# Six edits to the order of work around the FFNs, the first convolution steps on ScalarE, and the length of two down parts

## The chip, the cores and the metric

The kernel runs on one core of a Trainium2 chip. The metric is the device time of one execution in microseconds (us); lower is better. PE is TensorE, DVE VectorE, ACT ScalarE, POOL GpSimd, SP SyncE, which issues nearly all DMAs. A difference under 0.2% (6.8 us) can't be told from none here.

## The reference

Three parts, each over S = 1024 tokens of D = 1024 features in float32:

```python
for layer in range(2):                         # first block
    y = conv_lru_mixer(x) if layer == 0 else diff_attention_mixer(x)
    x = layer_norm(ALPHA * x + y)
    x = layer_norm(ALPHA * x + (silu(x @ w_gate) * (x @ w_up)) @ w_down)    # D_FF = 2816
mod = c_act @ w_ada + b_ada                    # second block: six rows of 1024
h = ln(x) * (1 + sc1) + sh1
x = ln_affine(ALPHA * x + (1 + g1) * (concat(mlstm(h), fourier(h)) @ w_out))
h2 = ln(x) * (1 + sc2) + sh2
out = ln_affine(ALPHA * x + (1 + g2) * (square(relu(h2 @ w_ff1 + b_ff1)) @ w_ff2 + b_ff2))  # 4096
```

The first mixer's A half is a causal depthwise convolution with 31 taps, over a gated projection, then a layer norm and silu; its B half a convolution with 4 taps before a gated linear recurrence.

## The kernel before

A class `Net` records all operations; a scheduler of the framework then sets each engine's order by its own costs, so the program's order is a wish and priority. Dependencies are kept by semaphores. Features lie on the 128 partitions; eight tiles of 128 tokens (`NTT = 8`).

**Matmuls.** Each float32 product is made of three matmuls. `split` (L213, L214) casts a tile to a rounded high part on ScalarE and subtracts it on VectorE for the low part; `mm3` (L235 to L237) multiplies high by high, low by high, high by low. A weight of 128x1024 is loaded to a `raw` buffer (a ring of three, `self.rp`), cast to `wh`, split to `wl`.

**The first mixer.** `conv` (L482 to L486) makes one half of a chunk: a first step `co = ga * w + b`, then 30 steps `co += shifted ga * w`, all on VectorE; 8 halves. `taps` (L503 to L506) does the same with 4 taps for 4 chunks `rc`. `prod_a` transposes `co` into `pt` (L576) and on.

**Gate and up.** They are made in pairs of features by seven products instead of eight, in `product` (L697 on). `prepare` makes from two weight tiles the combinations S1 to S4 (L674 to L677 on VectorE, then casts and splits); `xn.sums` (L150 to L153) makes from the tokens the combinations T1 to T4, where T1 to T4 of the second token half need the last tile. In `product`: `corner` A11B11 into `wx`, kept by a copy `keep`; S2T2 into `wy`, plus `keep`, copied to `u`; S1T1 into `wz`, copied to `p5`, plus `u`; S3T3 added into `wy`; `sum22` adds `wy` and `p5`; `corner2` A12B21 added into `wx`; S4B22 into `wz`; A22T4 into `wy`. Each of these terms is 12 matmuls. `start` begins the corner products of six pieces already while the mixer ends (`more` in the pipes of the three stages before; `EARLY` gives how many per call), since they need no sums.

**Down.** `run_ffn` makes the second product in parts of features: `PARTS1` for the first two FFNs, `PARTS2` for the third. For a part, `weights(j)` loads, casts and splits the weights of its features; kind "x" keeps them in tiles `wd` of the pool of 16 KB tiles, "u" in `wh`, `wl` of the large pool. Then for each token tile `tokens` loads the activations back from `hd` as `ht` (four features a load), `down_tile` multiplies into `dn`, and `add` adds that to `xr` (L898). The next part's weights come after the third tile (`WAHEAD`). In the last part, norm, transposes and the next stage's products follow in a pipe. In the second FFN, a side job runs along: `steps` issues w_ada loads of 512 KB, each followed by one reduction on VectorE (L1240), 48 in all, `SD` per product and `SDN` per down tile.

**Third FFN.** Its gate is `square(relu)`, L1821 on ScalarE and L1822 on VectorE. Its down weights are scaled by a row (L1828), and a bias row `b2` is scaled once (L1836) and added to each tile in its second part (L1844), both on GpSimd.

## Time and profile before

| | |
|---|---|
| median of 3 runs | 3423.69 us (3421.68 to 3425.16) |
| profiled execution | 3421.3 us, span 3419.5 us |
| mean granted clock of TensorE | 0.985 |
| PE busy | 3269.5 us, 96% |
| VectorE busy | 2185.5 us, 64% |
| ScalarE busy | 1412.9 us, 41% |
| GpSimd busy | 265.6 us, 8% |
| DMA share of 16 engines | 30.6%, 348.68 MB |

Times are us from the span's start. The first mixer lies at 0 to 370, the first FFN's gate and up to 758, its down to about 1040, attention to 1610, the second FFN's gate and up to 2055, its down with the second block's first norms to 2345, the second block's mixer to 2745, the third FFN's gate and up to 3054, its down to the end. PE is nearly full, so its gaps are what is read. A wait row names the waiting engine, tile and line, then the engine, tile and line that ended the wait. Where a wait is for several, it is put down to the one that came last.

### The profile page before, as it was taken

What the parts mean: (1) busy time and instruction counts of PE and PEld (TensorE: products, weight loads), DVE (VectorE), ACT (ScalarE), POOL (GpSimd) and SP (SyncE); (2) the same over time, 40 slices, a digit from 0 to 9 for tenths busy, and PEclk for the clock granted to TensorE, in tenths of its full rate; (3) what the DMA queues carried; (4) which work ended last, traced back from release to release, by engine and by line L of the source; (5) the groups of instructions that cost most, each with busy time, mean ns of one, the idle gap of its engine ahead of it and who ended that gap; (6) DMA issues with size and microseconds to landing.
All of it is one profiled execution on the core that took longest, in us unless ns stands there. A gap on an engine that the chain in (4) does not pass through costs nothing.

```text
span 3419.5 us, 40944 instructions
## 1 busy us (share of the span) xinstructions
PE 3269.5 (96%) x15588; PEld 2692.5 (79%) x15588; DVE 2185.5 (64%) x3445; ACT 1412.9 (41%) x2422; POOL 265.6 (8%) x458
## 2 busy tenths in 40 slices
PE   8998999999999999989999999999999989999998
PEld 7776788878877878877788878778777878878887
DVE  8997755555357677676765558654446876566635
ACT  4455433332237667655533332224334554432211
POOL 1011000000020111101000000013001300000201
PEclk9999999999999999999999999999999999999999
DMA  3131322235312111141332238721123333344312
GB/s 126 42 112 62 101 91 74 91 128 169 106 62 71 36 50 50 43 149 56 109 107 99 93 120 290 237 74 47 59 84 106 116 117 117 116 161 165 113 51 79
DMA packets 191764, 348.68 MB, mean 102 GB/s; under 512 B 14384, under 2 KB 105936, under 8 KB 191568
## 3 DMA queue, kind: packets, MB, share of 16 engines
q1 hardware_dynamic: 191568, 346.07, 30.6%
q8 instruction: 122, 2.00, 0.2%
q14 instruction: 74, 0.61, 0.1%
HBM read 268.41 MB, written 72.36 MB: 100 GB/s over the span
## 4 chain that ended last, share of the span: by engine, by line
PE 66%; DVE 13%; ACT 9%; DMA 5%; issue 4%; POOL 3%; SPq 0%; POOLq 0%; DVEq 0%; ACTq 0%
PE dn L236 6%; PE dn L235 6%; PE dn L237 6%; PE wy L235 4%; PE wy L236 4%; PE wy L237 4%; PE wx L235 3%; PE wx L237 3%; PE wx L236 3%; PE pi L235 3%; PE pi L236 3%; PE pi L237 2%; PE wz L235 2%; PE wz L237 2%; PE wz L236 2%
## 5 line engine op out<-in xcount | busy, mean ns | idle before, releaser
L213 ACT CAST wh<-raw 128x1024 fp32r<-128x1024 f32 (+1 forms) x275 | 282.7, 1048 | 405.1 <-DVE raw L677 138.1
L214 DVE TENSOR_TENSOR wl<-raw,wh 128x1024 fp32r<-128x1024 f32 (+1 forms) x275 | 334.3, 1233 | 132.1 <-ACT wh L213 128.1
L213 ACT CAST ht<-ht 128x512 fp32r<-128x512 f32 (+1 forms) x168 | 97.2, 580 | 448.0 <-DMA ht<-hd 438.7
L235 PE MATMUL dn<-wd,ht 128*128 128x512 f32 x704 | 274.4, 391 | 3.3 <-ACT wd L213 3.3
L236 PE MATMUL dn<-wd,ht 128*128 128x512 f32 x704 | 274.8, 390 | 1.3 <-DVE wd L214 1.2
L237 PE MATMUL dn<-wd,ht 128*128 128x512 f32 x704 | 274.4, 390 | 0.0
L235 PE MATMUL dn<-wh,ht 128*128 128x512 f32 x512 | 200.9, 392 | 10.8 <-DVE xr L898 6.7
L214 DVE TENSOR_TENSOR ht<-ht 128x512 fp32r<-128x512 f32 (+1 forms) x168 | 112.3, 673 | 153.2 <-ACT ht L213 152.4
L235 PE MATMUL wx<-bh,wh 128*128 128x512 f32 x480 | 192.2, 400 | 10.6 <-ACT keep L693 4.2
L237 PE MATMUL wx<-bh,wl 128*128 128x512 f32 x480 | 190.2, 397 | 11.2 <-DVE wl L214 11.2
L237 PE MATMUL dn<-wh,ht 128*128 128x512 f32 x512 | 200.3, 391 | 0.4 <-DVE ht L214 0.4
L236 PE MATMUL dn<-wl,ht 128*128 128x512 f32 x512 | 200.2, 391 | 0.0
L236 PE MATMUL wx<-bl,wh 128*128 128x512 f32 x480 | 190.3, 396 | 0.0
L235 PE MATMUL pi<-xh,wh 128*128 128x512 f32 x416 | 168.8, 406 | 7.8 <-DVE xl L214 7.8
L486 DVE SCALAR_TENSOR_TENSOR co<-ga,col,co 128x512 f32<-128x512 f32 (+18 forms) x240 | 165.4, 737 | 0.5
L237 PE MATMUL pi<-xh,wl 128*128 128x512 f32 x416 | 165.0, 397 | 0.0
L236 PE MATMUL pi<-xl,wh 128*128 128x512 f32 x416 | 164.9, 396 | 0.0
L235 PEld LDWEIGHTS dn<-wd,ht 128*128 128x128 f32 x704 | 132.3, 188 | 32.0 <-ACT wd L213 4.6
L236 PEld LDWEIGHTS dn<-wd,ht 128*128 128x128 f32 x704 | 132.4, 188 | 30.3 <-DVE wd L214 2.9
L237 PEld LDWEIGHTS dn<-wd,ht 128*128 128x128 f32 x704 | 132.4, 188 | 27.5
L287 POOL TENSOR_SCALAR nm<-sum 128x1 f32<-128x1 f32 x47 | 15.1, 322 | 1562.8 <-DVE xr L898 1323.1
L898 DVE SCALAR_TENSOR_TENSOR xr<-xr,dn 128x1024 f32<-128x1024 f32 x64 | 77.8, 1216 | 85.5 <-PE dn L237 81.3
(458 smaller groups left out, 8446.4 us busy)
## 6 DMA issues: line engine op xcount, KB each, us to landing
raw<-w_gu SPq DMA_DIRECT2D x100, 512.0 KB
hd<-g SPq DMA_DIRECT2D x152, 256.0 KB
raw<-w_f SPq DMA_DIRECT2D x70, 512.0 KB
ht<-hd SPq DMA_DIRECT2D x136, 256.0 KB
raw<-w_ada SPq DMA_DIRECT2D x48, 512.0 KB
raw<-w_dn SPq DMA_DIRECT2D x44, 512.0 KB
raw<-w_in SPq DMA_DIRECT2D x26, 512.0 KB
raw<-w_out SPq DMA_DIRECT2D x24, 512.0 KB
```

What stands on the lines that cost most here:

```text
L213: self.nc.scalar.copy(hi, src)
L214: (self.nc.gpsimd if pool else self.nc.vector).tensor_sub(lo, src, hi.bitcast(F32))
L235: mm(out, l[0], r[0], start=first, stop=False, **kw)
L236: mm(out, l[0], r[1], start=False, stop=False, **kw)
L237: mm(out, l[1], r[0], start=False, stop=last, **kw)
L287: (nc.vector if NMV else nc.gpsimd).tensor_scalar(nm, a, -1.0 / D, None, op0=ALU.mult)
L486: nc.vector.scalar_tensor_tensor(co[c][:, a:hi_], ga[c][:, a - s:hi_ - s], self.c("conv_w", 31 * c + 30 - s), co[c][:, a:hi_], op0=ALU.mul ...
L898: nc.vector.scalar_tensor_tensor(xr[i], xr[i], DN_ALPHA if first else 1.0, p, op0=ALU.mult, op1=ALU.add, accum_out=self.sum_of(xr[i]) if l ...
```

## The change

- A. The first step of `conv` and of `taps` is an activation (Identity with scale and bias) on ScalarE instead of a `tensor_scalar` on VectorE.
- B. In the pipes ahead of the three gate/up stages, `more` for the last tile stands ahead of `sums`.
- C. In `product`, `corner2` stands ahead of S3T3 instead of after `sum22`.
- D. `weights(0)`, the first down weights of each FFN, is called ahead of the last product instead of after it.
- E. `PARTS1` goes from 8x, 6u, 4x, 4u to 8x, 4u, 4x, 6u.
- F. The last part's `ht` in the first two FFNs comes from the `raw` ring of three instead of the large pool.
- G. `SDN`, w_ada steps per down tile, goes from 2 in all parts to 3, 1, 1, 0 by part.
- H. In the third FFN the scaling of `b2` and its eight additions go from GpSimd to VectorE.

```diff
@@ -28,7 +28,7 @@
 NF2 = 4096 // P
 NEG = -1.0e30
 EARLY, WAHEAD = (1, 1, 2, 2), 2
-PARTS1 = ((8, "x"), (6, "u"), (4, "x"), (4, "u"))
+PARTS1 = ((8, "x"), (4, "u"), (4, "x"), (6, "u"))
 PARTS2 = ((8, "x"), (6, "u"), (8, "x"), (6, "u"), (4, "x"))
 L2 = 2
 DV = 1
@@ -48,7 +48,7 @@
 WE, WP = 0, (0, 1)
 LM, MF, AF2, TF2 = 5, (3,4,5), (0,1,2), True
 NDB = (4, 4, 4, 4, 2, 2, 2, 2)
-SD, SDN, KA, KB = (0, 1), 2, 1, 3
+SD, SDN, KA, KB = (0, 1), (3, 1, 1, 0, 0), 1, 3
 FA, FB, FC = (3, 3, 3, 4, 4, 3, 2, 2), (4, 4, 4, 4, 1, 2, 2, 2), (2, 2, 2, 2, 1, 1, 1, 1)
 ND2 = (2,) * 8
 TS, TS0, TSM, T2 = True, False, True, 3
@@ -479,8 +479,8 @@
 
         def conv(c, h):
             lo_, hi_ = h * H512, (h + 1) * H512
-            nc.vector.tensor_scalar(co[c][:, lo_:hi_], ga[c][:, lo_:hi_], self.c("conv_w", 31 * c + 30),
-                                    self.c("conv_b", c), op0=ALU.mult, op1=ALU.add)
+            nc.scalar.activation(co[c][:, lo_:hi_], ga[c][:, lo_:hi_], AF.Identity, bias=self.c("conv_b", c),
+                                 scale=self.c("conv_w", 31 * c + 30))
             for s in range(1, 31):
                 a = max(lo_, s)
                 nc.vector.scalar_tensor_tensor(
@@ -500,8 +500,7 @@
         def taps(c):
             rec = recs[c]
             rc = rcs[c] = self.u("rc")
-            nc.vector.tensor_scalar(rc, rec, self.c("lconv_w", 4 * c + 3), self.c("lconv_b", c),
-                                    op0=ALU.mult, op1=ALU.add)
+            nc.scalar.activation(rc, rec, AF.Identity, bias=self.c("lconv_b", c), scale=self.c("lconv_w", 4 * c + 3))
             for s in range(1, 4):
                 nc.vector.scalar_tensor_tensor(rc[:, s:], rec[:, :S - s], self.c("lconv_w", 4 * c + 3 - s),
                                                rc[:, s:], op0=ALU.mult, op1=ALU.add)
@@ -632,7 +631,7 @@
             conv(c, 1)
         more = lambda i: start() if i == NTT - 1 else None
         self.pipe(pre + [(0, lambda i: feat(i - 4)), (LE, prod_a), (LE + ME[0], more), (LE + ME[1], more),
-                         (LE + ME[2], more), (LE + 1, norm), (LE + 2, feat), (LE + 3, xn.sums), (LE + 3, more)],
+                         (LE + ME[2], more), (LE + 1, norm), (LE + 2, feat), (LE + 3, more), (LE + 3, xn.sums)],
                   range(4, 8))
 
     def mixer_end(self, xr, xn, layer):
@@ -712,10 +711,10 @@
         p5 = self.tmp("p5")
         nc.scalar.copy(p5, pz)
         nc.vector.tensor_add(pz, pz, u2)
+        if not early:
+            self.corner2(o, x, px, finish)
         self.term(py, o["S3"], x, "T3", False, True)
         sum22(py, p5)
-        if not early:
-            self.corner2(o, x, px, finish)
         self.term(pz, o["S4"], x, "B22", False, True)
         finish(0, 1, pz)
         self.term(py, o["A22"], x, "T4", False, True)
@@ -788,20 +787,6 @@
         def prep(n):
             q, m = order[n]
             return self.prepare(src(2 * q, m), src(2 * q + 1, m), first=(q, m) not in started)
-
-        o = prep(0)
-        while begun:
-            finish_first()
-        for n, (q, m) in enumerate(order):
-            nxt = prep(n + 1) if n + 1 < len(order) else None
-            finish, sum22 = finisher(q, m)
-            self.product(o, x, keep(q, m), finish, sum22, (q, m) in started)
-            if m == nm - 1:
-                ctx.pop(q)
-            if n % 2:
-                kept.pop(n // 2)
-            o = nxt
-            steps(SD[n % 2])
 
         def weights(j):
             n, kind = parts[j]
@@ -818,13 +803,30 @@
                 ws.append((t[:, e, :], t[:, e + 1, :]))
             return ws
 
+        ws = {}
+        o = prep(0)
+        while begun:
+            finish_first()
+        for n, (q, m) in enumerate(order):
+            nxt = prep(n + 1) if n + 1 < len(order) else None
+            finish, sum22 = finisher(q, m)
+            if nxt is None:
+                ws[0] = weights(0)
+            self.product(o, x, keep(q, m), finish, sum22, (q, m) in started)
+            if m == nm - 1:
+                ctx.pop(q)
+            if n % 2:
+                kept.pop(n // 2)
+            o = nxt
+            steps(SD[n % 2])
+
         def tokens(j, i):
             n, hs = parts[j][0], []
             for a in range(0, n, 4):
                 e = min(n, a + 4)
                 shape = (P, 2, e - a, P)
                 if add_half is None and j == len(parts) - 1:
-                    t = self.u("ht", shape, F32R)
+                    t = self.rp.tile(list(shape), F32R, tag="raw", name=self.name("ht"))
                 else:
                     t = self.wp.tile(list(shape), F32R, tag="w", name=self.name("ht"))
                 raw = t[:, 1].bitcast(F32)
@@ -834,7 +836,7 @@
             return hs
 
         todo = [(j, i) for j in range(len(parts)) for i in range(NTT)]
-        ws, hs = {0: weights(0)}, {}
+        hs = {}
 
         def ahead(n):
             if n < len(todo) and todo[n] not in hs:
@@ -854,7 +856,7 @@
             for i in range(NTT):
                 h, w = before(j, i)
                 add(i, self.down_tile(i, h, w), j == 0, False)
-                steps(SDN)
+                steps(SDN[j])
             ws.pop(j)
         last = len(parts) - 1
         if side is not None:
@@ -1200,7 +1202,7 @@
         more = lambda i: start() if i == NTT - 1 else None
         sums = lambda i: xn.sums(i) if i >= 4 else None
         self.pipe([(0, lambda i: heads4(i, 4)), (LO + MO[0], more), (LO + 2, feat), (LO + 1, norm), (LO, o_prod),
-                   (LO + MO[1], more), (LO + MO[2], more), (LO + 3, sums), (LO + 3, more)])
+                   (LO + MO[1], more), (LO + MO[2], more), (LO + 3, more), (LO + 3, sums)])
 
     def ada(self):
         nc, A = self.nc, self.A
@@ -1810,7 +1812,7 @@
 
         stats = lambda i: self.ln_stats(xr[i])
         self.pipe([(3, stats), (4, stats), (1, prep), (3, norm1), (4, norm2), (2, prod)] + [(m, more) for m in MF]
-                  + [(LM, feat), (0, moments), (LM + 1, lambda i: xn.sums(i) if i >= 4 else None), (LM + 1, more)])
+                  + [(LM, feat), (0, moments), (LM + 1, more), (LM + 1, lambda i: xn.sums(i) if i >= 4 else None)])
 
     def block2_ff(self, x, xr, out):
         nc, A = self.nc, self.A
@@ -1833,7 +1835,7 @@
                 st["b2"] = self.u("b2")
                 r12 = ROWS.index("b_ff2")
                 nc.sync.dma_start(st["b2"], A["rows"][r12:r12 + 1, :].to_broadcast([P, D]))
-                nc.gpsimd.tensor_mul(st["b2"], st["b2"], st["g2"])
+                nc.vector.tensor_mul(st["b2"], st["b2"], st["g2"])
             xr.append(self.u("xr"))
             nc.sync.dma_start(xr[i], self.xs[2][blk(i), :])
 
@@ -1841,7 +1843,7 @@
             nc.vector.scalar_tensor_tensor(xr[i], xr[i], ALPHA2 if first else 1.0, p, op0=ALU.mult, op1=ALU.add,
                                            accum_out=self.sum_of(xr[i]) if last and S4 else None)
             if cnt[i] == 1:
-                nc.gpsimd.tensor_add(xr[i], xr[i], st["b2"])
+                nc.vector.tensor_add(xr[i], xr[i], st["b2"])
             cnt[i] += 1
 
         def add_half(i, p, cs):
```

**Order of instructions, A.** VectorE at the first convolution, from the gated values `ga` of the first half on (`co` is the sum, `wl` a weight split that the scheduler puts between). Before:

```order
L465 SCALAR_TENSOR_TENSOR ga_201<-pi_237,col,ga_201 128x512
L482 TENSOR_SCALAR co_205<-ga_201,col 128x512
L486 SCALAR_TENSOR_TENSOR co_205<-ga_201,col,co_205 128x511
L214 TENSOR_TENSOR wl_350<-raw_347,wh_349 128x1024
L486 SCALAR_TENSOR_TENSOR co_205<-ga_201,col,co_205 128x510
```

With the change:

```order
L465 SCALAR_TENSOR_TENSOR ga_201<-pi_237,col,ga_201 128x512
L486 SCALAR_TENSOR_TENSOR co_205<-ga_201,col,co_205 128x511
L486 SCALAR_TENSOR_TENSOR co_205<-ga_201,col,co_205 128x510
L214 TENSOR_TENSOR wl_350<-raw_347,wh_349 128x1024
L486 SCALAR_TENSOR_TENSOR co_205<-ga_201,col,co_205 128x509
```

And ScalarE in the same place with the change (`ga` L462 is the gate's sigmoid, `xh`, `wh` are casts):

```order
L462 ACTIVATE ga_201<-pi_211,col 128x512
L213 CAST xh_139<-xt_160 128x1024
L482 ACTIVATE co_205<-ga_201,col 128x512
L213 CAST wh_349<-raw_347 128x1024
L213 CAST wh_412<-raw_410 128x1024
```

The first step has left VectorE's row and stands on ScalarE behind the gate and one cast.

**Order of instructions, B.** VectorE at the first FFN's start, the last token tile `f_2631`: its sums `ts`, their splits `bl` and `bs`, the corner's weight split (`wl_2714`, with the change `wl_2698`), and the weight combinations (L674 to L677, with the change L673 to L676). Before:

```order
L151 TENSOR_TENSOR ts_2660<-f_2631,ts_2660 128x512
L152 TENSOR_TENSOR ts_2661<-f_2631 128x512
L153 TENSOR_TENSOR ts_2661<-f_2229,ts_2660 128x512
L887 TENSOR_TENSOR g_2619<-g_2619,wx_2593 128x512
L214 TENSOR_TENSOR bl_2448<-ts_2660,bh_2447 128x8x128
L214 TENSOR_TENSOR bs_2453<-ts_2661,bs_2451 128x2x128
L214 TENSOR_TENSOR bs_2454<-ts_2661,bs_2452 128x2x128
L214 TENSOR_TENSOR bs_2461<-ts_2661,bs_2459 128x2x128
L214 TENSOR_TENSOR bs_2462<-ts_2661,bs_2460 128x2x128
L214 TENSOR_TENSOR wl_2714<-raw_2711,wh_2713 128x1024
L214 TENSOR_TENSOR w_390_2755<-raw_2753,w_390_2755 128x512
```

With the change, from the tenth row behind `wl_2698` on (the nine between are splits of the tile before the last and a gate product):

```order
L214 TENSOR_TENSOR w_390_2755<-raw_2753,w_390_2755 128x512
L673 TENSOR_TENSOR raw_2753<-raw_2753 128x512
L674 TENSOR_TENSOR raw_2753<-raw_2751,raw_2753 128x512
L675 TENSOR_TENSOR raw_2751<-raw_2753,raw_2751 128x512
L676 TENSOR_TENSOR raw_2751<-raw_2751 128x512
L150 TENSOR_TENSOR ts_2729<-f_2631,f_2229 128x512
L152 TENSOR_TENSOR ts_2730<-f_2631 128x512
L151 TENSOR_TENSOR ts_2729<-f_2631,ts_2729 128x512
L214 TENSOR_TENSOR wl_2763<-raw_2751,wh_2762 128x1024
L153 TENSOR_TENSOR ts_2730<-f_2229,ts_2729 128x512
L214 TENSOR_TENSOR bl_2448<-ts_2729,bh_2447 128x8x128
L214 TENSOR_TENSOR bs_2453<-ts_2730,bs_2451 128x2x128
```

Before, the last corner's `wl` came behind the last `bl` and `bs`, and the weight combinations after that. Now `wl_2698` stands 20 rows ahead of the last `bl`, and the combinations and one S2 split stand ahead of the last `bl`, whose `bs` follow behind it.

**Order of instructions, D.** ScalarE in the third FFN's last product, from the copy `u` on (`wd` are down weights, `ht` down tokens, `g` the gate). Before:

```order
L709 COPY u_3824_23691<-wy_23677 128x512
L713 COPY p_3826_23706<-wz_23693 128x512
L1821 ACTIVATE g_23721<-g_23721,col 128x512
L1821 ACTIVATE g_23738<-wx_23663,col 128x512
L1821 ACTIVATE g_23738<-wz_23693,col 128x512
L213 CAST ht_23830<-ht_23830 128x512
L1821 ACTIVATE g_23721<-wy_23677,col 128x512
L213 CAST wd_23777<-raw_23774 128x1024
L213 CAST wd_23777<-raw_23780 128x1024
L213 CAST wd_23788<-raw_23785 128x1024
```

With the change:

```order
L708 COPY u_3837_23737<-wy_23723 128x512
L213 CAST wd_23668<-raw_23665 128x1024
L213 CAST wd_23668<-raw_23671 128x1024
L213 CAST wd_23679<-raw_23676 128x1024
L712 COPY p_3839_23752<-wz_23739 128x512
L1823 ACTIVATE g_23767<-wx_23709,col 128x512
L213 CAST wd_23679<-raw_23682 128x1024
L1823 ACTIVATE g_23783<-g_23783,col 128x512
L1823 ACTIVATE g_23767<-wz_23739,col 128x512
L213 CAST wd_23690<-raw_23687 128x1024
L213 CAST ht_23830<-ht_23830 128x512
L213 CAST wd_23690<-raw_23693 128x1024
```

The first three casts of `wd` stand right behind `u`, ahead of the copy `p`, and the rest between the squares; before, all of them came behind the last `g`.

## Rows read from the trace of the kernel before

**Rows 1.** The page: busy time of each engine over the span.

```profile
PE 3269.5 (96%) x15588; PEld 2692.5 (79%) x15588; DVE 2185.5 (64%) x3445; ACT 1412.9 (41%) x2422; POOL 265.6 (8%) x458
```

**Rows 2.** Waits of PE over the whole span: us in total, times, longest.

```profile
PE wx L237 <- DVE wl L214: 11.2, 3, 4.5
PE pt L576 <- DVE co L486: 10.1, 2, 9.9
...
PE pi L235 <- DVE xl L214: 7.8, 1, 7.8
...
PE wy L235 <- ACT u L709: 5.7, 5, 2.1
PE pv L235 <- ACT xh L213: 4.3, 1, 4.3
...
PE dn L235 <- ACT wd L213: 3.3, 2, 2.5
...
PE dn L236 <- DVE wd L214: 1.2, 2, 0.8
```

**Rows 3.** Windows: length, busy us (instructions) by engine PE PEld DVE ACT POOL, clock, DMA, GB/s.

```profile
24.00:294.00 270.00, 252.31 (x1081) 200.56 (x1079) 264.35 (x354) 117.95 (x141) 17.48 (x24) 0.97 0.22 73
287.00:302.00 15.00, 4.26 (x23) 3.89 (x23) 10.78 (x19) 3.46 (x8) 1.48 (x4) 0.54 0.00 1
```

**Rows 4.** Timeline of PE: start us, duration; two of four corner2 matmuls, then S3T3.

```profile
465.64 0.39 PE L237 MATMUL wx<-bh,wl 128*128 128x512 f32 x1
465.87 0.39 PE L235 MATMUL wx<-bh,wh 128*128 128x512 f32 x1
466.24 0.50 PE L235 MATMUL wy<-bs,wh 128*128 128x512 f32 x1
466.57 0.40 PE L236 MATMUL wy<-bs,wh 128*128 128x512 f32 x1
```

**Rows 5.** Timeline of PE at the end of the convolutions.

```profile
294.64 0.69 PE L576 MATMUL pt<-ident,co 128*128 128x128 f32 x2 [9.86 <-DVE co L486]
```

**Rows 6.** Source lines: duration ns min/median/max, first and last start us, shape.

```profile
L482 DVE TENSOR_SCALAR co<-ga,col x8: 512/540/548, 25.2 to 254.7; 128x512 f32<-128x512 f32 x8
...
L503 DVE TENSOR_SCALAR rc<-rec,col x4: 802/806/811, 46.1 to 157.9; 128x1024 f32<-128x1024 f32 x4
...
L494 ACT ACTIVATE rec<-pi,col x8: 678/690/690, 39.1 to 153.4; 128x512 f32<-128x512 f32 x8
...
L306 ACT ACTIVATE xr<-xr,nm,rs x24: 1239/1244/1283, 239.9 to 1628.8; 128x1024 f32<-128x1024 f32 x24
```

**Rows 7.** Timeline of the start of the first FFN.

```profile
364.07 1.21 DVE L214 TENSOR_TENSOR wl<-raw,wh 128x1024 fp32r<-128x1024 f32 x1
...
365.34 0.50 PE L237 MATMUL wx<-bh,wl 128*128 128x512 f32 x1 [3.82 <-DVE wl L214]
...
365.92 0.69 DVE L674 TENSOR_TENSOR raw<-raw 128x512 f32<-128x512 f32 x1
...
372.82 0.39 PE L235 MATMUL wy<-bh,wh 128*128 128x512 f32 x1
```

**Rows 8.** Timeline of PE: the first S2T2 of the third FFN.

```profile
2776.51 0.39 PE L235 MATMUL wy<-bh,wh 128*128 128x512 f32 x1
```

**Rows 9.** Timeline of PE in the last product of the first FFN.

```profile
755.24 0.50 PE L235 MATMUL wy<-bs,wh 128*128 128x512 f32 x1 [1.85 <-ACT u L709]
```

**Rows 10.** Windows of down parts, columns as in rows 3.

```profile
2055.00:2142.00 87.00, 87.00 (x386) 72.03 (x385) 70.59 (x91) 21.10 (x27) 0.00 (x0) 1.00 0.86 289
2251.00:2345.00 94.00, 81.61 (x414) 69.42 (x413) 55.46 (x81) 42.60 (x84) 26.41 (x58) 0.93 0.21 71
980.00:1045.00 65.00, 56.36 (x328) 48.98 (x329) 41.26 (x65) 35.07 (x63) 17.68 (x25) 0.97 0.24 80
```

**Rows 11.** Timelines of SyncE and ScalarE: a token load issued, and its cast.

```profile
2223.08 5.80 SPq L831 DMA_DIRECT2D ht<-hd  x2
...
2227.71 0.62 ACT L213 CAST ht<-ht 128x512 fp32r<-128x512 f32 x1 [2.51 <-DMA ht<-hd]
```

## The prediction

> **What bounds the kernel now.** I read the page first: TensorE (PE) is busy 96% of the span, VectorE 64%, ScalarE 41%, GpSimd 8% [rows 1]. Time can only go where PE stands idle or runs at the half clock. The list of PE's waits is next [rows 2]; these lie at the change's places: `wx` behind the weight split `wl`, 11.2 us in 3 waits; `pt` behind the convolution `co`, 10.1 us; `wy` behind the copy `u`, 5.7 us; `dn` behind `wd`, 3.3 and 1.2 us; and the two drains at a stage's end, `pi` behind `xl` 7.8 us and `pv` behind `xh` 4.3 us. Third come stretches: in the 15 us around the long wait for `co` the mean granted clock is 0.54 [rows 3], near the lower of its two levels, 1.2 of 2.4 GHz. So a long wait costs itself and some slow matmuls behind it.
>
> **The change part by part.** The letters are those of the list of the change.
>
> *A, first steps of the convolutions on ScalarE.* VectorE bounds this stretch: from 24 to 294 us it is busy 264.35 of 270 us [rows 3], and at its end PE has waited 9.86 us for the last accumulation step [rows 5]. Taken from VectorE: 8 x 0.540 + 4 x 0.806 = 7.5 us [rows 6]. ScalarE takes the steps up. The nearest rows are Identity at 0.690 us on 128x512 and an activation at 1.244 us on 128x1024 [rows 6], thus 8 x 0.69 + 4 x 1.244 = 10.5 us on an engine that is busy 118 of those 270 us. But each first step is now a hand-over, and ScalarE takes it only in its order, behind instructions that wait for PE. At the very first chunk VectorE has no other step to do, about 1 us lost (a ScalarE step less the removed one, and the way there and back); later, other halves and chunks fill in, as the order shows. Bounds: 0 (all of it handed back), and 7.5 + 2 us (half of the slow part of those 15 us goes too). The nearest row is VectorE's idle time, under 6 of 270 us: almost nothing waits there for others, so most of the 7.5 stays. I take **5**.
>
> *B, corner products before the last sums.* At the start of each gate/up stage PE stands for `wl`: 3.82 us in the first [rows 7], 4.5 us at the longest [rows 2], so 2.9 in the one left over. In the order before, VectorE splits the sums' `bl` and four `bs` first, and only then makes `wl`. The change puts `wl` ahead of the last token tile's sums. Yet these have still to be made: the first S2T2 needs `bl` of that tile. In the new order, ahead of that `bl` and behind `wl`, there stand the earlier tile's `bl` and `bs`, a split `w`, four weight combinations of 0.69 us [rows 7], four sums and another `wl`. Against the old order, where sums and `wl` were done at 365.28 [rows 7], VectorE has 0.68 + 4 x 0.69 = 3.4 us more to do before that `bl`: some 368.7. PE had 20 matmuls left when it stopped, 3.82 us before 365.34; at 0.227 us it would be at S2T2 at 366.1. So 2.6 us of wait come back one product later. S2T2 began at 372.82 [rows 7] and now begins about 368.7: 4.1 us, less 1 for slow matmuls behind the new wait, so 3. The second start has the same order: 3. In the third, the weight combinations stay behind the sums and the same VectorE work lies ahead of S2T2, which came at 2776.51 [rows 8]: 1. Sum **7**; bounds 0 (all comes back later) and 11.2 plus 3 for the slow matmuls.
>
> *C, A12B21 before S3T3.* S3T3 accumulates into `wy`, from which `u` is still being copied. In every second product four corner matmuls stand ahead of it, and PE still loses 0.37 + 0.33 - 2 x 0.23 = 0.24 us there [rows 4]; 21 such places (8, 8 and 5) are 5. In the last products of the first two stages the wait is 1.85 us [rows 9] and 2.1 [rows 2], with a slower first matmul 2.1 and 2.4. Twelve matmuls ahead, 12 x 0.23 = 2.8 us, cover each. What is uncovered in turn: behind S3T3 only S4B22, 2.8 us, now covers the sum that the last term waits for, one VectorE operation of 0.69 us in VectorE's order. Products that were started early have that distance already, and no such wait is among the larger ones. Sum 9.5, I take **9**; bounds 5 (only the steady places) and 10.
>
> *D, the first down weights before the last product.* All of PE's waits for `wd` are one place, the third FFN's first down tile: 3.3 + 1.2 = 4.5 us [rows 2], and slow matmuls behind, some 6 in all. The casts now stand between `u` and the last squares on ScalarE, as the order shows, with six terms of PE's work (16 us) around them. The scaling of the bias row goes to VectorE too, ahead of the last `wd` split. Between 0 and 6 I take **3.5**.
>
> *E and F, parts of 8, 4, 4, 6, and the last part's tokens on the raw ring.* Six features give PE 36 matmuls, 8.2 us a tile, where four gave 5.4, so more work beside the norm of the tile before. In the first FFN's end PE is idle 65 - 56.36 = 8.6 us, in the second's 94 - 81.61 = 12.4 us [rows 10]: the most that can be had, with 1 or 2 us of clock. The last tile's chain still drains. Against it, the tokens leave a large pool for three raw buffers. A load takes 4.6 us from issue to landing [rows 11], with cast and split of 0.62 and 0.68 us 5.9, and a tile has two. One load can be under way while two are read, and 8.2 us cover it. I take **4** for the first FFN (bounds -3 to 10) and **4.5** for the second (-3 to 14).
>
> *G, w_ada steps.* In the second FFN's first part each of 8 tiles takes three loads of 512 KB instead of two, 8 more, but only four weights of the next part are loaded instead of six. Six loads more are 3.1 MB; at the rate of the rows, 289 GB/s at a share of 0.86, so 336 when full, that is 9.4 us, against 0.14 x 87 = 12 us free [rows 10]. VectorE goes from 70.6 by 8 x 1.3 to 81 of 87 us. It fits, narrowly: **-1**, bounds -6 and 3.
>
> *H, the bias on VectorE.* Nine operations like those of 1.2 us, 11 us in the last down stage, over 300 us long, in a kernel where VectorE is busy 64%. **0**; if the cover fails, one operation at a few tiles: -3.
>
> **The sum.** 5 + 7 + 9 + 3.5 + 4 + 4.5 - 1 = 32 us. From the profiled execution's 3421.3 that gives 3389.3; it lies 2.4 us under the median of 3423.69, so for the median I forecast **3391**.
>
> A rule of the Trainium skill speaks against A: "ScalarE: Activation LUTs", section "Rules for kernel authors", wants additions and multiplications on VectorE. The rows agree on the price of one operation, 0.690 against 0.540 us. By the rule the sum would be without A's gain.
>
> **The rivals.**
> 1. *The convolution gets no shorter* (that rule as a mechanism): each chain begins behind ScalarE, 8 x 0.15 + 4 x 0.44 = 3 us longer instead of 5 gained: 3399. For it: ScalarE is in order and waits for PE. Against: other chunks fill in. 0.07.
> 2. *The sums are merely late elsewhere*: PE waits at the first S2T2 for all that it saved at `wl`, B gives 0: 3398. For it: the same VectorE work precedes. Against: at 365.34 PE still had 20 matmuls to do, which now go first. 0.12.
> 3. *The last part starves on three buffers* (slower). If weights of the next stage hold one of the three, a tile's second load is issued only when the tile before lets go: 5.9 us against 2.8 of cover, 3.1 at each of 16 tiles, 50 us, and E and F's 8.5 are gone: 3450; from 8 tiles on it decides against the kernel. For it: one queue issues all these loads in order. Against: at 8.2 us a tile most loads lie a tile ahead. 0.06.
> 4. *The first part becomes DMA's*: new waits in G at the lower bound, 5 us more: 3396. 0.08.
> 5. *Gaps are only refilled*: the next engine in line holds PE at most places, a fifth of the sum stays: 3417. 0.07.
>
> **Numbers.** My forecast has 0.60; its own range is 3380 to 3402. Rivals 1, 2 and 4 lie inside that. Down to 3376 if slow matmuls vanish at more places; up to 3411 for two parts that fail together. Rivals 3 and 5 stay out. A measurement of this kernel can tell 0.2%, 6.8 us, from no change: faster 0.60 + 0.07 + 0.12 + 0.08 = 0.87; within it 0.07 (rival 5); slower 0.06 (rival 3).
>
> **What would show it.** A: `pt` behind `co` 3 to 5 us instead of 9.86. B: no `wx` behind `wl`, but a wait of 2 to 3 us of `wy` for `bl` in the first two stages. C: no `wy` behind `u` over 1 us in a last product. D: `dn` behind `wd` under 1.5 us in all. E: the drains `pi` and `pv` under 5 and 3 us. G: the second FFN's first part still 87 us. I am wrong if `dn` behind `ht` grows over 10 us, or if span less PE's busy time, 150 us now [rows 1], falls by less than 15.

## The result and the profile after

The changed kernel takes 3382.12 us (median of 4 runs, 3380.67 to 3382.69), against 3423.4 us before in the same session. The ratio is 0.9879, 95% interval 0.9862 to 0.9896: 41 us less (36 to 47). The forecast was 3391, range 3376 to 3411. The profiled execution's span is 3380.0 us, 39.5 us less.

The page's first part after; compare [rows 1]:

```profile
PE 3251.7 (96%) x15588; PEld 2685.6 (79%) x15588; DVE 2172.7 (64%) x3442; ACT 1426.2 (42%) x2434; POOL 246.6 (7%) x449
```

PE executes the same 15588 matmuls and transposes. Its idle time, span less busy, falls from 150 to 128.3 us, by 21.7. Its busy time falls by 17.8 us although nothing was removed: these are matmuls that no longer run at a lower clock or slowly behind a wait. The mean granted clock rose from 0.985 to 0.990; and with C undone alone, PE is busy for 3260.1 us at the same 0.990, so C's places make up some of the 17.8 without the clock.

The waits of PE over the span after, the lines that answer to [rows 2] and the new ones (us in total, times, longest):

```profile
PE dn L235 <- DVE xr L900: 11.4, 6, 5.9
...
PE pi L235 <- ACT wh L213: 4.6, 1, 4.6
...
PE pt L575 <- DVE co L486: 3.6, 2, 3.4
...
PE pv L235 <- ACT wh L213: 3.2, 2, 1.8
...
PE wy L235 <- ACT wh L213: 2.9, 1, 2.9
...
PE wy L235 <- ACT u L708: 2.4, 3, 1.1
...
PE wy L235 <- ACT bh L213: 0.9, 2, 0.5
...
PE dn L235 <- ACT wd L213: 0.7, 1, 0.7
...
PE dn L236 <- DVE wd L214: 0.6, 1, 0.6
```

`wx` behind `wl`, 11.2 us before, is gone. `pt` behind `co` has 3.6 left of 10.1, `wy` behind `u` 2.4 of 5.7, `wd` 1.3 of 4.5. The drain `pi` has 4.6 of 7.8, now behind the cast of a weight, `wh`. One line grew: `dn` behind `xr`, to 11.4 us with one wait of 5.9, from this line before:

```profile
PE dn L235 <- DVE xr L898: 6.7, 5, 2.8
```

It comes back below.

Where the time went, stage by stage: the start of the first matmul of each place in the two profiled executions (us), and how much earlier it is after.

| first matmul of | before | after | earlier |
|---|---|---|---|
| first FFN, corner (`wx`) | 328.96 | 320.08 | 8.9 |
| first FFN, S2T2 (`wy`) | 372.82 | 358.11 | 14.7 |
| first FFN, down | 766.25 | 748.91 | 17.3 |
| second FFN, corner | 1623.89 | 1603.26 | 20.6 |
| second FFN, S2T2 | 1667.38 | 1640.42 | 27.0 |
| second FFN, down | 2060.31 | 2030.49 | 29.8 |
| second block, `pi` after the last norm | 2336.37 | 2305.36 | 31.0 |
| third FFN, corner | 2723.33 | 2691.91 | 31.4 |
| third FFN, S2T2 | 2776.51 | 2742.66 | 33.9 |
| third FFN, down | 3054.35 | 3017.45 | 36.9 |
| last `dn` | 3407.26 | 3367.27 | 40.0 |

So 8.9 us are A's, 5.8, 6.3 and 2.4 lie where B works, 2.6, 2.9 and 3.1 in the products (C, D), 3.3 between the first FFN's down and the second's corner (E, F), 3.1 in the third FFN's down (D, H). The second FFN's down, where E, F and G meet, gives only 1.2.

### The profile page after: what moved, and what is told of

The parts are those of the page before. It is cut to its first block, busy times and chain, and to the rows that moved or that the text cites. A ratio compares the mean times of both kernels' runs of the same rounds, so it can differ in the third digit from the quotient of the medians.

```text
span 3380.0 us, 40969 instructions
## 1 busy us (share of the span) xinstructions
PE 3251.7 (96%) x15588; PEld 2685.6 (79%) x15588; DVE 2172.7 (64%) x3442; ACT 1426.2 (42%) x2434; POOL 246.6 (7%) x449
## 4 chain that ended last, share of the span: by engine, by line
PE 63%; DVE 16%; ACT 9%; DMA 6%; issue 4%; POOL 3%; SPq 0%; DVEq 0%; POOLq 0%; ACTq 0%
PE dn L237 6%; PE dn L235 6%; PE dn L236 6%; PE wy L236 4%; PE wy L237 4%; PE wy L235 4%; DVE co L486 3%; PE wz L235 3%; PE wx L235 3%; PE wx L236 3%; PE wx L237 3%; PE wz L236 2%; PE wz L237 2%; PE pi L235 2%; PE pi L236 2%
## 5 line engine op out<-in xcount | busy, mean ns | idle before, releaser
L486 DVE SCALAR_TENSOR_TENSOR co<-ga,col,co 128x512 f32<-128x512 f32 (+21 forms) x240 | 163.7, 736 | 1.2 <-ACT co L482 0.9
L235 PEld LDWEIGHTS dn<-wh,ht 128*128 128x128 f32 x512 | 96.6, 189 | 34.7 <-issue 7.8
```

Source lines behind the costliest of these rows:

```text
L235: mm(out, l[0], r[0], start=first, stop=False, **kw)
L486: nc.vector.scalar_tensor_tensor(co[c][:, a:hi_], ga[c][:, a - s:hi_ - s], self.c("conv_w", 31 * c + 30 - s), co[c][:, a:hi_], op0=ALU.mul ...
```

## Experiments

Twelve kernels were run, most of them the changed kernel with one part undone. Each was timed against the kernel before in its own session; where a difference to the changed kernel is given in us, it is the difference of the two ratios times 3423. These intervals are nearly 6 us wide on either side, and the difference of two of them some 8. By the times alone, then, only B, E with F, F, and the two better versions at -16 differ clearly from the change; a single part is read from where in the profile the shift begins, and that is one execution of each kernel. Undone one at a time (E and F together), the parts add up to some 28 of the 41 us.

| kernel | median us | ratio to before | interval | against the change |
|---|---|---|---|---|
| the change | 3382.12 | 0.9879 | 0.9862 to 0.9896 | |
| A undone | 3387.67 | 0.9894 | 0.9879 to 0.9909 | +5 |
| B undone | 3392.52 | 0.9906 | 0.9891 to 0.9921 | +9 |
| C undone | 3387.90 | 0.9893 | 0.9878 to 0.9908 | +5 |
| D undone | 3385.19 | 0.9880 | 0.9863 to 0.9897 | 0 |
| E and F undone | 3391.78 | 0.9909 | 0.9892 to 0.9925 | +10 |
| F undone | 3371.11 | 0.9850 | 0.9834 to 0.9866 | -10 |
| G undone | 3379.01 | 0.9870 | 0.9856 to 0.9885 | -3 |
| w_ada earlier | 3376.52 | 0.9864 | 0.9849 to 0.9878 | -5 |
| H undone | 3382.84 | 0.9886 | 0.9868 to 0.9903 | +2 |
| F undone, w_ada earlier | 3363.16 | 0.9832 | 0.9816 to 0.9847 | -16 |
| the same, D in the third FFN only | 3362.63 | 0.9832 | 0.9815 to 0.9850 | -16 |
| F undone, w_ada earlier, C undone | 3373.63 | 0.9857 | 0.9841 to 0.9874 | -8 |

### A undone

```diff
-            nc.scalar.activation(co[c][:, lo_:hi_], ga[c][:, lo_:hi_], AF.Identity, bias=self.c("conv_b", c),
-                                 scale=self.c("conv_w", 31 * c + 30))
+            nc.vector.tensor_scalar(co[c][:, lo_:hi_], ga[c][:, lo_:hi_], self.c("conv_w", 31 * c + 30),
+                                    self.c("conv_b", c), op0=ALU.mult, op1=ALU.add)
...
-            nc.scalar.activation(rc, rec, AF.Identity, bias=self.c("lconv_b", c), scale=self.c("lconv_w", 4 * c + 3))
+            nc.vector.tensor_scalar(rc, rec, self.c("lconv_w", 4 * c + 3), self.c("lconv_b", c),
+                                    op0=ALU.mult, op1=ALU.add)
```

> The changed kernel with A undone (first steps of both convolutions back on VectorE). If VectorE's own time bounds the first mixer, the 7.5 us come back there, the wait of pt for co grows from 3.4 us to 9 or 10 us, and the first wx starts 8 to 9 us later than in the changed kernel (at some 329 us): 3382 + 8.5 = 3390.5. Rival: the shift of 8.9 us came from elsewhere in the stage (order, clock), and undoing A gives back under 4 us: below 3386.

The wait is back, in the list of PE's waits with A undone:

```profile
PE pt L576 <- DVE co L486: 10.1, 2, 9.8
```

and the first corner product starts at 328.62 us, 8.5 later than with the change. That is no scatter: in the profiles of all twelve kernels with A it starts at 318.8 to 321.3. VectorE is busy 264.71 us of 24 to 294; with the change, in a window that is 8 us shorter (columns as in [rows 3]):

```profile
24.00:286.00 262.00, 250.63 (x1082) 198.97 (x1080) 257.36 (x343) 130.36 (x154) 15.89 (x24) 0.99 0.22 75
```

That is 7.0 us less work than in [rows 3] and as full: 257.36 of 262 us, so little was lost in the hand-overs to ScalarE. There the first steps of `conv` take longer than the row that the prediction took for them, 0.817 us, and VectorE waited for one of them once, 0.9 us (second line, from the list of who waited):

```profile
L482 ACT ACTIVATE co<-ga,col x8: 817/817/819, 24.9 to 145.7; 128x512 f32<-128x512 f32 x8
...
  DVE co L486: 0.9, 1
```

The theory holds for the stage. In total, the profiled execution, the slowest of its four, is 10.7 us longer, although its second FFN's down took 3.6 us less, by a smaller wait of the kind described under G; by the times some 5 us came back.

### B undone

```diff
-                         (LE + ME[2], more), (LE + 1, norm), (LE + 2, feat), (LE + 3, more), (LE + 3, xn.sums)],
+                         (LE + ME[2], more), (LE + 1, norm), (LE + 2, feat), (LE + 3, xn.sums), (LE + 3, more)],
...
-                   (LO + MO[1], more), (LO + MO[2], more), (LO + 3, more), (LO + 3, sums)])
+                   (LO + MO[1], more), (LO + MO[2], more), (LO + 3, sums), (LO + 3, more)])
...
-                  + [(LM, feat), (0, moments), (LM + 1, more), (LM + 1, lambda i: xn.sums(i) if i >= 4 else None)])
+                  + [(LM, feat), (0, moments), (LM + 1, lambda i: xn.sums(i) if i >= 4 else None), (LM + 1, more)])
```

> The changed kernel with B undone (sums ahead of the last corner products in all three pipes). My theory: the stretch from the first wx to behind the first S1T1 gets longer by 4.5, 4.5 and 1.5 us in the three stages, with waits of wx for wl of 3 to 4.5 us: 3382 + 10.5 = 3392.5. Rival (the prediction's sizes): 3 + 3 + 1 = 7: 3389. Rival that the order of VectorE alone is at work and the sums come late anyway: under 3 us, 3385.

PE's waits with B undone show the three of before:

```profile
PE wx L237 <- DVE wl L214: 11.3, 3, 4.5
```

S2T2 starts later, measured from the corner's start and against the change, by 7.2, 4.9 and 2.6 us in the three stages. Some of that is made up in the products that follow: at the first down matmul 5.9, 4.1 and 2.3 us remain, 12 in sum. By the times B is worth 9 us, between the theory of 10.5 and the prediction's 7, which they can't separate; the profile is nearer to the theory.

How the wait that the prediction expected in its place turned out shows in the timeline of the changed kernel at the first FFN's S2T2 (start us, us; compare [rows 7]):

```profile
357.01 1.04 ACT L213 CAST bh<-ts 128x1024 fp32r<-128x1024 f32 x1
...
357.26 0.39 PE L237 MATMUL wx<-bh,wl 128*128 128x512 f32 x1
...
358.11 0.50 PE L235 MATMUL wy<-bh,wh 128*128 128x512 f32 x1 [0.46 <-ACT bh L213]
358.28 1.22 DVE L214 TENSOR_TENSOR bl<-ts,bh 128x1024 fp32r<-128x1024 f32 x1
...
359.05 0.51 PE L235 MATMUL wz<-bh,wh 128*128 128x512 f32 x1 [0.45 <-ACT wh L213]
...
359.56 0.50 PE L236 MATMUL wy<-bl,wh 128*128 128x512 f32 x1
```

`bl` is there at 359.50; the count had 368.7, less A's 8.9 us 359.8. But S2T2's first matmul needs only `bh`, from ScalarE, and a matmul of S1T1 goes in between, so PE waits three times about half a microsecond: from 357.49, where the next matmul was due, to 359.56 it started two, and 1.6 us are lost, not 2.6. And the clock didn't fall:

```profile
335.00:365.00 30.00, 29.04 (x129) 23.00 (x128) 28.31 (x49) 19.21 (x42) 0.00 (x0) 1.00 0.29 97
```

The second stage's S2T2 starts with the same two short waits. In the third, PE waits for 2.9 us, and not for `bl` but for the cast of S2T2's weight: it is the line `wy` behind `wh` in the list of waits above. The prediction did not have this wait, and the stage gained 2.4 us all the same.

### C undone

```diff
-        if not early:
-            self.corner2(o, x, px, finish)
         self.term(py, o["S3"], x, "T3", False, True)
         sum22(py, p5)
+        if not early:
+            self.corner2(o, x, px, finish)
```

> The changed kernel with C undone (corner2 after sum22). My theory: small waits of S3T3 come back, 8 x 0.25, 8 x 0.25 and 5 x 0.25 us, and 2.1 and 2.4 us in the last products of the first two FFNs: 3382 + 9.7 = 3391.8. Rival: D gives the last products other work, so that their waits don't come back: + 5.3, 3387.4.

The waits came back, more than was expected (`wy` behind `u` stood at 2.4 us with the change):

```profile
PE dn L235 <- DVE xr L900: 7.7, 7, 2.4
PE wy L235 <- ACT u L708: 7.1, 5, 2.8
```

3387.90 is the rival's number, but not for its reason: in the last products of the first two FFNs PE waits for `u` again, 2.8 and 1.8 us. Between S2T2 and the down stage 5.2 us are lost in the first FFN, 5.9 in the second, 2.5 in the third. At the steady places, S3T3 begins as in [rows 4], one matmul late and the next one slow, with C undone:

```profile
453.03 0.39 PE L235 MATMUL wx<-bh,wh 128*128 128x512 f32 x1
453.41 0.50 PE L235 MATMUL wy<-bs,wh 128*128 128x512 f32 x1
453.75 0.40 PE L236 MATMUL wy<-bs,wh 128*128 128x512 f32 x1
```

From one S2T2 to the next such a product takes some 19.32 us, with the change 19.04: 0.26 to 0.29 us at each of the 21 places. The last products of the first two FFNs take 2.7 and 3.3 us longer than with the change, up to the first down matmul. Together that is 11.7 us; the rest of the third FFN's 2.5 lies in its first product, which takes 13.2 us here, 11.6 with the change, but 13.8 with H undone, where C stands. In the second FFN's down, on the other side, this execution is 6.2 us shorter than the change's: `dn` behind `xr` falls from 11.4 to 7.7 us, and of its 5.9 us wait there none over 1.8 is left. Whether that belongs to C is not shown: this stage takes 259.4 to 263.7 us in the five kernels that keep C, E, F and G (the change, and A, B, D or H undone), and 256.9 here. The last kernel below looks at it again.

### D undone

```diff
-            if nxt is None:
-                ws[0] = weights(0)
...
+        ws[0] = weights(0)
```

> The changed kernel with D undone (first down weights after the last product). My theory: dn waits for wd 4.5 us at the third FFN's first tile, with slow matmuls behind it, against 1.3 us in the changed kernel: 3382 + 5 = 3387. Rival: H moved the bias row to VectorE behind the same splits and makes it worse, + 7: 3389. Rival: with C the last product leaves VectorE and ScalarE free anyway, + 2: 3384.

PE's waits from 3010 us on with D undone:

```profile
PE dn L235 <- ACT wd L213: 2.2, 1, 2.2
PE dn L236 <- DVE wd L214: 1.7, 1, 1.7
PE dn L235 <- DVE xr L1842: 0.8, 1, 0.8
```

In the third FFN, from S2T2 to the last `dn`, 7.8 us are lost: 2.2 before the first down matmul and 5.6 in the down stage, though the waits add up to 4.7 us against 1.3. But this execution came to that stage 4.9 us earlier than the changed kernel, and its four runs spread from 3377.82 to 3386.94. By the times the difference can't be told from none. The gain in the third FFN stands in the profile: its down stage takes 349.1 to 351.1 us in the eleven profiled executions with D and H there, and 355.4 with D undone. What D costs elsewhere is not shown.

### E and F undone, and F alone

```diff
-PARTS1 = ((8, "x"), (4, "u"), (4, "x"), (6, "u"))
+PARTS1 = ((8, "x"), (6, "u"), (4, "x"), (4, "u"))
...
-                    t = self.rp.tile(list(shape), F32R, tag="raw", name=self.name("ht"))
+                    t = self.u("ht", shape, F32R)
```

> The changed kernel with E and F undone (parts 8, 6, 4, 4; the last part's tokens from the large pool), w_ada still at 3, 1, 1. My theory: the tails come back, some 3 us at the first FFN's end (drain of pv 4.3 us) and, at the second's, waits for ht and a drain of pi of 4 and 8 us; but the second FFN's second part has six features a tile, so its wait of 5.9 us for xr goes. First FFN +3, second FFN +7 - 5 = +2: 3387. Rival: w_ada alone makes the 5.9 us, it stays and the tail is added: 3392. Rival: the parts' new lengths are worth nothing in the second FFN or cost there: 3382 or less.

The tails are back, in PE's waits with E and F undone:

```profile
PE pi L235 <- DVE xl L214: 6.8, 1, 6.8
PE pv L235 <- ACT xh L213: 4.5, 2, 4.3
PE dn L235 <- ACT ht L213: 4.4, 1, 4.4
```

By the times E and F together are worth 10 us, near the forecast (8.5); 3391.78 is the first rival's number. As that rival has it, the wait for `xr` stays, 10.4 us in all, though its longest, 3.8, now lies in the second FFN's first part. For F alone the second of the two edits was undone:

> The changed kernel with F alone undone: the last part's tokens from the large pool again, parts 8, 4, 4, 6 kept. If three raw buffers cost waits in the last parts, the waits dn behind xr of 2.4 us at the first FFN's end and pv behind wh of 1.8 and 1.3 us go: 3382 - 3 = 3379. If the ring is wide enough, nothing moves: 3382. If the large pool is too full for six features (its tiles hold back other tiles), slower: 3386.

The surprise of the study: without F the kernel is 10 us faster than with it. From the first FFN's first down matmul to the second FFN's corner it gains 7.4 us, in the second's down 3.2. The queue of SyncE, which issues the loads in order, shows why. Its waits from 880 to 1010 us, with the change:

```profile
SPq L833 <- PE dn L237: 74.5, 14, 37.6
...
SPq L218 <- DVE wl L214: 8.1, 2, 4.1
```

and without F:

```profile
SPq L218 <- DVE wl L214: 33.7, 3, 12.8
SPq L833 <- PE dn L237: 22.4, 6, 7.8
```

L833 is the load of `ht`, L218 that of a weight. On the ring of three L833 waits 74.5 us for `dn` matmuls to let a buffer go, 14 times, up to 37.6 us; from the large pool 22.4 us, 6 times. Behind it stand the weights of the attention, which use the same ring; without F their own wait for splits to free a buffer is 33.7 us, with it 8.1. PE's first matmul of their kind (`pv`) starts at 976.83 us with the change, behind a wait for `wh`, and at 957.78 without F. PE is busy in the windows of the two ends, with the change and without F (columns as in [rows 3]):

```profile
950.00:1012.00 62.00, 55.00 (x292) 46.21 (x291) 36.49 (x56) 31.32 (x54) 12.83 (x20) 1.00 0.30 101
```

```profile
900.00:1000.00 100.00, 99.30 (x493) 84.09 (x492) 47.04 (x69) 36.00 (x60) 12.62 (x29) 1.00 0.20 69
```

7 us of 62 idle, against 0.7 of 100. With w_ada earlier, F costs 11 us as well (the better version below). The edit takes back the shared ring and the number of buffers at once; a ring of three for the tokens alone, or another queue, wasn't tried, so which of these costs the 10 us stays open. E alone, then, from E and F undone to F undone, is worth 3391.78 - 3371.11 = 20.7 us by the medians (20 by the ratios), and F costs half of it. In the two profiles E's 18 us lie where it works: 9.5 from the first FFN's down to the second's corner, 8.7 from the second's down to the third's corner.

### G undone, and w_ada earlier

```diff
-SD, SDN, KA, KB = (0, 1), (3, 1, 1, 0, 0), 1, 3
+SD, SDN, KA, KB = (0, 1), (2, 2, 2, 2, 2), 1, 3
```

> The changed kernel with G undone: w_ada steps 2 per down tile in every part, now with a second part of only four features, 5.4 us a tile. My theory: the second part's 43 us then carry 16 w_ada loads instead of 8, and PE waits there more: the wait for xr of 5.9 us grows to 10 us or more, the first part has more room: 3382 + 4 = 3386. Rival: the 5.9 us come from three w_ada loads a tile in the first part, which leave its successor's weights late; with two they go: 3377.

The theory fails, since the wait doesn't grow; the rival, at 3377, is near 3379.01, but -3 us lies inside the interval. The single wait of 5.9 us falls apart into 1.2, 1.5, 0.8 and 0.9 us; all of `dn` behind `xr` in the second FFN's down is 4.9 us, against 7.9, and that stage is 4.5 us shorter. Then the loads were moved ahead of the down stage, into gate and up:

```diff
-SD, SDN, KA, KB = (0, 1), (3, 1, 1, 0, 0), 1, 3
+SD, SDN, KA, KB = (1, 1), (2, 1, 1, 0, 0), 1, 3
```

> The changed kernel with w_ada steps moved out of the down parts into gate and up: one step per product (SD 1, 1 instead of 0, 1), then 2, 1, 1 per down tile. 22 of 48 loads then lie in the gate/up stage, where DMA is at a third and VectorE at 59%. My theory (DMA in the second FFN's first two parts makes the 5.9 us wait): that wait falls under 2 us, gate and up gets no new wait, 3382 - 5 = 3377. Rival: the wait is of the weights' ring of three raw buffers and VectorE's order, not of the load: unchanged, 3382. Rival: w_ada steps in each product delay the weights' splits in gate and up and cost there: 3386.

PE's waits over the span there:

```profile
PE dn L235 <- DVE xr L900: 4.0, 4, 2.4
PE wy L235 <- ACT u L708: 4.0, 5, 1.1
```

`dn` behind `xr` falls from 11.4 to 4.0 us, and none of it over 0.5 us lies in the second FFN's down, which is 10.9 us shorter; `wy` behind `u` grows by 1.6 us, and gate and up is 3.5 us longer. What the wait was shows in the changed kernel's timeline of ScalarE, VectorE and PE before it ended:

```profile
2123.69 1.04 ACT L213 CAST wd<-raw 128x1024 fp32r<-128x1024 f32 x1 [1.43 <-DMA raw<-w_dn]
...
2124.77 1.23 DVE L214 TENSOR_TENSOR wd<-raw,wd 128x1024 fp32r<-128x1024 f32 x1 [1.24 <-ACT wd L213]
2125.82 1.04 ACT L213 CAST wd<-raw 128x1024 fp32r<-128x1024 f32 x1 [0.56 <-DMA raw<-w_dn]
...
2126.89 1.23 DVE L214 TENSOR_TENSOR wd<-raw,wd 128x1024 fp32r<-128x1024 f32 x1 [0.30 <-ACT wd L213]
2128.04 1.22 DVE L900 SCALAR_TENSOR_TENSOR xr<-xr,dn 128x1024 f32<-128x1024 f32 x1
...
2129.40 0.77 PE L235 MATMUL dn<-wh,ht 128*128 128x512 f32 x1 [5.92 <-DVE xr L900]
```

The addition of `xr`, which frees the `dn` that PE needs, stands on VectorE behind splits of `wd` for the part after; these wait for casts, and the casts for loads from `w_dn`, which share queue, ring and engines with w_ada. The windows of the first and second part with the change (columns as in [rows 3]):

```profile
2025.00:2112.00 87.00, 87.00 (x384) 71.91 (x385) 72.24 (x97) 18.70 (x24) 0.00 (x0) 1.00 0.89 293
2112.00:2160.00 48.00, 40.41 (x165) 31.83 (x164) 37.49 (x50) 14.00 (x17) 0.00 (x0) 0.93 0.87 274
```

The first part held, PE 87 of 87 us; the second paid, 40 of 48, with DMA at 0.87. In the four kernels with w_ada moved out none of these waits is over 0.8 us there, so w_ada's loads make it. G undone leaves 32 of them in the two parts, as the change does, but 16 and 16 instead of 24 and 8, and waits less: it may be the first part's third load a tile that leaves the weights behind it late, as the rival says; no run separates that from the sum. The wait's size scatters otherwise: 3.6 us with A undone, 6.9 with B, 5.3 with D, 4.8 with F, 3.4 with H undone.

### H undone

```diff
-                nc.vector.tensor_mul(st["b2"], st["b2"], st["g2"])
+                nc.gpsimd.tensor_mul(st["b2"], st["b2"], st["g2"])
...
-                nc.vector.tensor_add(xr[i], xr[i], st["b2"])
+                nc.gpsimd.tensor_add(xr[i], xr[i], st["b2"])
```

> The changed kernel with H undone (bias row and its eight additions on GpSimd again). Theory: VectorE is under half busy in the last down stage and nothing moves at the end; at the third FFN's first tile VectorE is 1.2 us earlier with the last wd split, so dn behind wd loses at most 0.6 us: 3382 - 0.5 = 3381.5. Rival: GpSimd's additions of 2.7 us hold back the next part's sums: + 2 to 3, 3385.

By the times no difference can be told (+2, intervals overlap). In the profiled execution, the slowest of its four, the third FFN's down is 6.2 us longer, with more waits than the change has:

```profile
PE dn L235 <- ACT wd L213: 1.5, 2, 0.8
PE dn L236 <- DVE wd L214: 1.4, 2, 0.8
PE dn L235 <- DVE xr L1843: 0.7, 1, 0.7
```

3.6 us in place of 1.3, and the granted clock behind them is lower, as the first 63 us of the stage show, with H undone and with the change (columns as in [rows 3]):

```profile
3013.40:3076.40 63.00, 60.05 (x248) 47.74 (x248) 43.95 (x43) 19.81 (x26) 2.87 (x1) 0.95 0.70 240
```

```profile
3014.40:3077.40 63.00, 61.73 (x272) 50.44 (x271) 44.62 (x45) 19.91 (x27) 0.00 (x0) 1.00 0.71 242
```

The stage's 356.0 us lie outside the 349.1 to 351.1 of the eleven executions with D and H, so H may be worth more than nothing; but before, with neither of the two, it took 352.9. Whether H saves this in each run stays open.

### The better version, and two kernels beside it

The second edits of the two sections above, F undone and w_ada earlier, together:

> The changed kernel without F (tokens of the last part from the large pool) and with w_ada steps moved into gate and up (SD 1, 1; SDN 2, 1, 1). If the two gains are of different places they add: no_f -8.5 at the first FFN's end, -2.5 in the second; the early w_ada -9 in the second's down, + 3 in its gate and up, some of it shared: 3382 - 8.5 - 7 = 3366. Rival: both take the same wait in the second FFN: 3370.

3363.16 us, 0.9832 of before (0.9816 to 0.9847), 16 us ahead of the change: the two add up. PE's waits there:

```profile
PE pi L235 <- ACT wh L213: 4.3, 1, 4.3
...
PE wy L235 <- ACT u L708: 3.1, 5, 1.3
...
PE dn L235 <- DVE xr L900: 2.0, 5, 0.7
```

Then with the first down weights ahead of the last product in the third FFN only:

```diff
-            if nxt is None:
+            if nxt is None and nf == NF2:
                 ws[0] = weights(0)
...
+        if 0 not in ws:
+            ws[0] = weights(0)
```

> As best1, and the first down weights ahead of the last product in the third FFN only (D undone in the first two). no_d was up to 4 us ahead of the changed kernel from the first FFN to the second's end, and behind it by 5.6 only from the third's first down tile. If that lead is D's cost on loads, 2 us more than best1: 3364. Rival: the lead was run to run scatter of the loads: equal to best1.

3362.63: the same. The lead of 4.9 us seen with D undone was scatter of the loads, or is worth nothing here. Last, C undone in the better version:

> best1 with C undone. In the changed kernel, C undone lost 5.2 and 5.9 us up to the second FFN's down parts, and won 6.2 us back there, where PE then waited less for xr. Theory: that was the loads' pace in those parts (the loads run on while PE is late); with w_ada moved out there is nothing to win back, and C is worth its full 5.2 + 5.9 + 2.4 = 13.5 us: 3363 + 13 = 3376. Rival: the win of 6 us comes from the weights' order in the last product itself, and stays: 3363 + 7 = 3370.

3373.63 us, +10.5 by the medians; in the profiles +12.1 (3374.6 against 3362.6 us of span). `wy` behind `u` is 9.1 us there:

```profile
PE wy L235 <- ACT u L708: 9.1, 8, 2.7
...
PE dn L235 <- DVE xr L900: 0.6, 2, 0.4
```

By the ratios it is +8.6. The time lies midway between the theory (3376) and the rival (3370) and settles neither. In the second FFN's down this kernel is only 1.1 us shorter than the better version, where C undone in the changed kernel was 6.2 shorter, as the theory wants. But by the times C's 5 us there and its 8.6 here can't be told apart, and B undone came to that stage 9 us late without any gain in it. That what comes early is handed back to the w_ada loads is thus argued, not shown. C is worth 9 to 12 us: 11.7 by the places in the changed kernel, 8.6 to 12 in the better version.

## Why the prediction was right

The time lies in the range, 9 us under the forecast (whose terms add up to 3391.7, put down as 3391), and the direction and most of the mechanisms were as said. Some of the nearness is luck: F, held to be free, costs 10 us, and E brings that much more than was said. By its steps:

- **A** was 5, measured 8.5 to 8.9 in its stage. The step that was mis-sized is "almost nothing waits there for others, so most of the 7.5 stays": all of it stayed, with 1.0 to 1.4 us on top. VectorE remained full; the wait for `co` fell to 3.4 us, inside the 3 to 5 that were named. The first rival, drawn from ScalarE's longer step, is out: a step takes 0.817 us on ScalarE, more than the 0.690 that was read, against 0.540 on VectorE [rows 6], and yet VectorE waited for them only once, 0.9 us. "ScalarE: Activation LUTs" of the Trainium skill, section "Rules for kernel authors", sends such work to VectorE; it would have kept it on the engine that was full here, and the measurement decides.
- **B** was 7, measured 9 by the times, 12 by the places. The count on VectorE to `bl` was good. Two sizes were off: PE lost 1.6 us and not 2.6 to the new wait in the first stage, and the slow matmuls that were charged behind it did not come. In the third the wait was another, for a weight's cast. The second rival (the sums merely late) is out.
- **C** was 9. By the places it is worth 11.7, over the bound of 10; by the times some 5, with a second FFN's down that is 6 us shorter when C is undone, for a reason that stays open. The steady places were sized well, 0.26 to 0.29 us at each of 21, 5.8 in sum, where the prediction read 0.24 from one [rows 4]. The mis-sized term are the last products of the first two stages: 2.7 and 3.3 us, not 2.1 and 2.4.
- **D** was 3.5. In the third FFN the profile shows up to 7.8 us, with the slow matmuls, over the bound of 6; in total time it can't be told.
- **E and F** were 8.5 together, measured 10. Right in sum by luck, from two errors that cancel. "One load can be under way while two are read, and 8.2 us cover it" failed: the ring is shared with the attention's weights, and one in-order queue carries both, so F costs 10 us. It did not show as `dn` behind `ht`, the sign that was named, but as `dn` behind `xr` and `pv` behind `wh`, 2.4, 1.8 and 1.3 us at the first FFN's end, which are gone without F. That is the third rival's mechanism at a fifth of its price. E is worth 18 to 20, about as much as the 21 us of idle time in [rows 10], where the prediction took 4 and 4.5 for E and F together.
- **G** was -1, measured -3 (not beyond the interval); against the earlier w_ada its stage is 10.9 us longer. "It fits, narrowly" held for the first part, where it was worked out, and not for the second, which has now 5.4 us a tile; that part was not worked out. The fourth rival named the cause; the wait came one part later than it said.
- **H** at 0 stands by the times; in one profile the stage is 6.2 us longer without it.

Besides, the slow clock was underrated: the mean granted clock rose from 0.985 to 0.990, and 17.8 of the 39.5 us are busy time. Some 5.8 of these are C's steady places, which the records show as busy and the sum had; for the rest it had only small shares beside each wait.

Of the signs named: `pt` behind `co`, no `wx` behind `wl`, no `wy` behind `u` over 1 us in a last product, `wd` at 1.3 us, the drain `pi` at 4.6, the first part at 87 us and the idle time held. The waits at S2T2 in the first two stages were shorter than said, and `pv` waits 3.2 us in all, over the 3 named.

## What to carry to other kernels

Where an engine is full, a step moved off it can come back in full, even if it takes longer on the other engine (8.5 us here for 7.5 us of steps), as long as the full engine has other pieces to go on with. Before tiles are moved to a small ring, look at who else lives on it and at the queue that fills it: here loads that waited for a buffer, 74.5 us in sum, held up the loads behind them, of the next stage too. And undo each part by itself: two parts that were priced as one, E and F, came out near their sum while one of them cost 10 us.

## What the runs showed that was not expected

- Nearly half of the gain is busy time: the same 15588 operations of PE took 17.8 us less, since fewer ran behind a wait or at a lower clock.
- The second FFN's down has a new wait behind its loads, 5.9 us in the changed kernel, 3.4 to 6.9 with another part undone, at most 1.8 with C undone, 1.5 with G undone, and under 0.8 in the four kernels with w_ada earlier. Why C bears on it stays open.
- Kernels that differ little spread differently: four runs of the change within 2 us, of D undone within 9.
